# A two-layer hybrid trunk on one core: recurrence gates in blocks of 80 channels, rotated scores stacked in float32r, another order of steps

## The chip, the cores and the metric

The kernel runs on one core of one Trainium2 chip. The metric is device time in microseconds (us) of one launch, the median over the runs shown. The profile is one execution of the program, taken by the hardware profiler.

Engines go by the profile's names: PE is TensorE (matrix products; PEld is its loading of the stationary operand), DVE is VectorE, ACT is ScalarE, POOL is GpSimd and SP is SyncE, whose queue issues nearly all DMAs of this kernel.

## The reference

Two layers act on 256 tokens of 1024 channels. In each, one large projection of the normed input feeds three mixers (a gated MLP over positions, attention with 8 heads, a linear recurrence), and their outputs are gated, projected, merged and added to the input:

```python
def mla_attention(c_q, c_kv, k_rope_in, ...):        # per head: 128 plain + 64 rotated channels
    ...
    q = jnp.concatenate([q_nope, q_rope], axis=-1)
    k = jnp.concatenate([k_nope, broadcast(k_rope)], axis=-1)
    s = jnp.einsum('bqhd,bkhd->bhqk', qi, k) * scale   # masked by chunks, softmax, times v
...
def rg_lru(x_c, conv_w, conv_b, w_a, b_a, w_x, b_x, lam):
    xc = depthwise_conv(x_c, conv_w) + conv_b             # 1280 channels, width 4
    xb = xc.reshape(B, S, 16, 80)                         # 16 blocks of 80 channels
    r = sigmoid(einsum('bshi,hij->bshj', xb, w_a) + b_a)
    i = sigmoid(einsum('bshi,hij->bshj', xb, w_x) + b_x)
    a = exp(-8 * r * softplus(-lam))
    h = scan(a, sqrt(1 - a*a) * i * xc)                   # h[t] = a[t] h[t-1] + b[t]
...
for l in range(2):
    h = rmsnorm(x); proj = h @ w_in[l]
    ...
    merged = sig(g_a) * (y_a @ w_proj_a) + sig(g_b) * (y_b @ w_proj_b) + sig(g_c) * (y_c @ w_proj_c)
    x = x + rmsnorm(merged @ w_out[l])
```

## The kernel before, in words

**Number format.** A float32 product is made of float32r products: each operand is split into a rounded high part (an ACT copy, `act(hi, src, AF.Copy)`) and a rest (a DVE subtraction), and `mm3` issues three products, high by high, high by low and low by high. Plain float32 operands go to PE unsplit in the scores and in the products with the softmax weights.

**Weights.** The weights are cut into chunks, mostly 1 MB (1024 rows by 256 columns, 48 products of 256 moving columns on PE). `load` issues a chunk's DMA on SP into one of three `raw` buffers; `split` makes `whi` and `wlo` from it in one of three pairs. When a step has used its chunk, `done` (through `fin`) gives the pair back, and `pump` splits the next chunk into it and issues the load of the third chunk after that. So PE has up to two split chunks ahead of the one it uses, and up to three more are loaded or loading.

**The order.** All steps of a layer stand in the table `ORDER`; the program is issued in just that order on every engine, with no rearrangement. `LATE` says at which point inside a step the chunk is given back. A step name has a number: `("ga", 2)` is the third chunk of gate a. The names that matter here: `xc` projects the recurrence's input, `conv` convolves it, `split` and `stack` prepare it for the gates, `la` and `lx` make its gates r and i, `r1`, `r2`, `r3` are the recurrence itself; `uq` and `ukv` make queries, keys and values, `attend i` issues the scores of heads 2i and 2i+1 and the later parts of the two pairs before; `u`, `za`, `zb`, `zc`, `ga` to `gc` and `pa` to `pc` are the other projections; `v` and `norm` belong to the gated MLP.

**The scores.** A head's scores take, for queries 0 to 127 (128 keys) and for queries 128 to 255 (256 keys), one float32 product of the plain part (`q`, `k`) and one of the rotated part (`qr`, `krt`). `qr` holds two heads over 128 partitions, and the two `krt` tiles have zeros where the other head's channels are.

**The gates.** The 1280 channels lie in two groups of five tiles of 128 partitions, which the blocks of 80 don't match. So `load` puts the blocks piece by piece (16 DMAs per chunk, after a POOL memset) into a sparse band of weights, and `lru_gate` covers each tile of 128 outputs by one full `mm3` plus either one product over 96 stacked partitions or another `mm3`. `conv_stack` copies the needed edges of the split input into `xs` and `xm`, on DVE, ACT and POOL. A step `la` or `lx` has 24 products of 256 columns; a layer has four such steps.

PSUM is used as a ring of five banks `mm` and one of three `aux`; small temporaries are a ring of eight tiles `t`; larger ones are 16 slots taken in turn.

## Time and profile before

| | |
|---|---|
| median of 3 runs | 798.14 us (798.09 to 798.59) |
| the profiled execution: time, span of its instructions | 798.34 us, 796.6 us |
| PE busy, DVE busy, ACT busy, POOL busy | 788.1, 548.9, 469.3, 70.5 us |
| granted TensorE clock, mean | 0.997 |
| moved by DMA, mean rate | 137.87 MB, 173 GB/s |
| written to HBM | 1.05 MB |

Busy times are sums over the instructions of an engine; instructions on PE overlap, so that the time of one product is read from the distance of two starts and not from its duration. In the rows below, a line number such as L731 is one of the kernel before; a row of a float32 (not float32r) product counts two records for one instruction.

### The profile page before, as it was taken

The numbers are of one execution on the slowest core, as the hardware profiler recorded it, in microseconds if no ns is written. First come the engines' busy times: TensorE is split into PE (matmuls) and PEld (weight loads), VectorE is DVE, ScalarE is ACT, GpSimd is POOL, SyncE is SP. The second block draws the span as 40 slices with busy tenths as digits, with TensorE's granted clock in tenths as the row PEclk, the third lists the DMA queues.
The fourth block names the chain that finished last, engine by engine and source line by source line (L and its number), as shares of the span: only waits on it lengthen the run. The fifth ranks groups of instructions, "written<-read, shape, count | busy, mean of one in ns | idle before, by whom it ended". The sixth has DMA issues, their size and how long they took to land.

```text
span 796.6 us, 15355 instructions
## 1 busy us (share of the span) xinstructions
PE 788.1 (99%) x6445; PEld 780.2 (98%) x6445; DVE 548.9 (69%) x712; ACT 469.3 (59%) x689; POOL 70.5 (9%) x110
## 2 busy tenths in 40 slices
PE   9999999999999999999999999999999999999996
PEld 8999999999999999999999999999999999999996
DVE  5587788666876787555666868776578578775562
ACT  5785767339855736343567776654595584544441
POOL 1100503003000000000010032031210000000000
PEclk9999999999999999999999999999999999999998
DMA  7845454344666565666357626541575656564531
GB/s 229 290 152 182 153 161 155 112 122 137 201 213 211 159 215 169 199 212 216 109 171 239 208 94 211 159 128 51 166 219 167 221 162 202 185 214 150 193 132 54
DMA packets 134205, 137.87 MB, mean 173 GB/s; under 512 B 11046, under 2 KB 130808, under 8 KB 134136
## 3 DMA queue, kind: packets, MB, share of 16 engines
q1 hardware_dynamic: 134120, 136.90, 54.3%
q8 instruction: 50, 0.82, 0.4%
q14 instruction: 19, 0.16, 0.1%
q10 hardware_dynamic: 16, 0.00, 0.0%
HBM read 135.83 MB, written 1.05 MB: 172 GB/s over the span
## 4 chain that ended last, share of the span: by engine, by line
PE 94%; DMA 2%; issue 1%; DVE 1%; ACT 1%; SPq 0%; POOL 0%; POOLq 0%; DVEq 0%; ACTq 0%
PE mm L308 25%; PE mm L307 25%; PE mm L309 25%; PE mm L431 2%; PE mm L433 2%; PE mm L432 2%; DMA raw<-in_w_in_dram 1%; PE aux L843 1%; PE mm L730 1%; PE aux L770 1%; PE mm L731 1%; DMA X<-in_x_dram 1%; PE mm L549 1%; PE aux L1021 1%; PE mm L1020 1%
## 5 line engine op out<-in xcount | busy, mean ns | idle before, releaser
L269 DVE TENSOR_TENSOR wlo<-raw,whi 128x2048 fp32r<-128x2048 f32 (+5 forms) x123 | 264.6, 2156 | 115.9 <-ACT whi L268 115.5
L307 PE MATMUL mm<-hT,whi 128*128 128x256 f32 x1088 | 307.1, 282 | 0.0
L309 PE MATMUL mm<-hT,wlo 128*128 128x256 f32 x1088 | 305.8, 281 | 0.3 <-DVE wlo L269 0.3
L308 PE MATMUL mm<-hT,whi 128*128 128x256 f32 x1088 | 305.6, 281 | 0.0
L268 ACT ACTIVATE whi<-raw 128x2048 fp32r<-128x2048 f32 (+5 forms) x123 | 221.0, 1802 | 66.6 <-PE mm L308 26.8
L309 PEld LDWEIGHTS mm<-hT,wlo 128*128 128x128 f32 x1088 | 205.0, 188 | 0.5 <-DVE wlo L269 0.5
L307 PEld LDWEIGHTS mm<-hT,whi 128*128 128x128 f32 x1088 | 205.0, 188 | 0.0
L308 PEld LDWEIGHTS mm<-hT,whi 128*128 128x128 f32 x1088 | 205.0, 188 | 0.0
L973 ACT ACTIVATE t<-mm 128x512 f32<-128x512 f32 x18 | 10.8, 598 | 52.2 <-PE mm L309 52.2
L397 POOL TENSOR_TENSOR rstd<-rstd,mhalf 128x1 f32<-128x1 f32 x8 | 4.4, 551 | 391.1 <-DVE rstd L396 391.1
L308 PE MATMUL mm<-yc,whi 128*128 128x256 f32 x128 | 36.0, 282 | 0.0
L308 PE MATMUL mm<-ya,whi 128*128 128x256 f32 x128 | 36.0, 282 | 0.0
L307 PE MATMUL mm<-ya,whi 128*128 128x256 f32 x128 | 36.0, 281 | 0.0
L307 PE MATMUL mm<-yc,whi 128*128 128x256 f32 x128 | 36.0, 281 | 0.0
L431 PE MATMUL mm<-whi,hT 128*128 128x256 f32 x128 | 36.0, 281 | 0.0
L308 PE MATMUL mm<-yb,whi 128*128 128x256 f32 x128 | 35.9, 281 | 0.0
L309 PE MATMUL mm<-ya,wlo 128*128 128x256 f32 x128 | 35.9, 280 | 0.0
L309 PE MATMUL mm<-yc,wlo 128*128 128x256 f32 x128 | 35.9, 280 | 0.0
L309 PE MATMUL mm<-yb,wlo 128*128 128x256 f32 x128 | 35.8, 280 | 0.0
L307 PE MATMUL mm<-yb,whi 128*128 128x256 f32 x128 | 35.8, 280 | 0.0
L432 PE MATMUL mm<-wlo,hT 128*128 128x256 f32 x128 | 35.8, 279 | 0.0
L433 PE MATMUL mm<-whi,hT 128*128 128x256 f32 x128 | 35.7, 279 | 0.0
(279 smaller groups left out, 1663.4 us busy)
## 6 DMA issues: line engine op xcount, KB each, us to landing
raw<-in_w_in_dram SPq DMA_DIRECT2D x76, 1024.0 KB
raw<-in_w_proj_a_dram SPq DMA_DIRECT2D x8, 1024.0 KB
raw<-in_w_proj_b_dram SPq DMA_DIRECT2D x8, 1024.0 KB
raw<-in_w_proj_c_dram SPq DMA_DIRECT2D x8, 1024.0 KB
raw<-in_w_out_dram SPq DMA_DIRECT2D x8, 1024.0 KB
raw<-in_mla_w_uq_dram SPq DMA_DIRECT2D x8, 576.0 KB
raw<-in_mla_w_ukv_dram SPq DMA_DIRECT2D x4, 1024.0 KB
raw<-in_w_in_dram SPq DMA_DIRECT2D x4, 640.0 KB
```

What stands on the lines that cost most here:

```text
L268: act(hi[:, w], c.raw[:, w], AF.Copy)
L269: V.tensor_tensor(lo[:, w], c.raw[:, w], f(hi[:, w]), ALU.subtract)
L307: mm(ps, lh, rh, start=start, stop=False)
L308: mm(ps, lh, rl, start=False, stop=False)
L309: mm(ps, ll, rh, start=False, stop=stop)
L431: mm(ps, lh, rh, start=k == 0, stop=False)
L432: mm(ps, lh, rl, start=False, stop=False)
L433: mm(ps, ll, rh, start=False, stop=k == KT - 1)
L549: mm(ps, ll, rh, start=False, stop=j % 2 * 4 + k == KT - 1)
L730: mm(sc[:, P : 3 * P], qn[:, P:], kn, start=True, stop=False)
L731: mm(sc[:, P : 3 * P], qp[:, P:], kr, start=False, stop=True)
L973: act(sg, ps, AF.Sigmoid)
```

## The change

There are four parts.

- **Gates by blocks.** A chunk `lg` now has four blocks of 80 channels of both `w_a` and `w_x`. The split input is stored to DRAM tiles (`split`, now one ACT copy, one DVE subtraction and two stores) and read back by blocks (`stack`): 80 high rows and, under them, 48 low rows of the block in one tile; the 80 high rows again and the other 32 low rows in a second. Each block then takes two products, over 128 and over 112 partitions, with 80 output rows. The biases go into the sigmoid of 80 partitions, from a layout by blocks; the sigmoids are stored to DRAM as well, and the new step `in` reads them back in tiles of 128 channels for `r1`. Weights come by six DMAs per chunk, of 80, 48 and 48 rows by 4 by 80, without a memset.
- **Scores.** The rotated query of a head is kept as 64 high and 64 low rows of one float32r tile (`qr`, now two tiles of four heads; two ACT copies and two DVE subtractions more in each `uq` step), and the key as two float32r tiles: `krt[0]` has its high part twice, `krt[1]` its rest twice. The rotated float32 product becomes two float32r products.
- **Order.** `ORDER` is rewritten: four steps `lg` in place of `la` and `lx`, `in` after every second one, and other places for `conv`, `split`, `stack`, `attend`, `zc`, `gb` and `pc`.
- **Constants.** The bias rows are loaded by 16 blocks of 80; the `rows` tile is cleared from row 64 on POOL.

```diff
 ORDER = (
-    ("wl", 0), ("xc", 0), ("turn", 0), ("xc", 1), ("conv", 0), ("uq", 0), ("conv", 1), ("xc", 2), ("ukv", 0),
...
+    ("xc", 0), ("wl", 0), ("turn", 0), ("xc", 1), ("conv", 1), ("uq", 0), ("conv", 0), ("xc", 2), ("xc", 3),
...
+    ("split", 1), ("pa", 0), ("ga", 1), ("lg", 1), ("in", 0), ("pa", 1), ("ga", 2), ("stack", 2), ("pa", 2),
+    ("r1", 0), ("ga", 3), ("r2", 0), ("pa", 3), ("zb", 0), ("stack", 3), ("lg", 2), ("zb", 1), ("zb", 2),
+    ("zb", 3), ("r3", 0), ("gb", 0), ("pb", 0), ("lg", 3), ("in", 1), ("gb", 2), ("gb", 1), ("pb", 1), ("r1", 1),
+    ("r2", 1), ("pb", 2), ("zc", 0), ("zc", 1), ("rows", 0), ("r3", 1), ("zc", 2), ("zc", 3), ("zc", 4), ("gc", 0),
...
 def load(c, parts=1, mid=None):
...
+        l, g = c.lru
+        for i, x in enumerate("ax"):
+            at = slice(i * WH, (i + 1) * WH)
+            w = I["lru_w_" + x][l, g * NH : (g + 1) * NH].rearrange("b r c -> r b c")
+            r1, r2 = v2(c.raw[:, at], BW), v2(c.raw[:, W2 + i * WH : W2 + (i + 1) * WH], BW)
+            nc.sync.dma_start(r1[:BW], w)
+            nc.sync.dma_start(r1[BW:], w[:K1])
+            nc.sync.dma_start(r2[64 : BW + K2], w[K1 - (BW - 64) :])
...
         if c.lru:
+            raw, r2 = c.raw[:, :W2], c.raw[64 : BW + K2, W2 : 2 * W2]
+            act(hi[:, :W2], raw, AF.Copy)
+            act(lo[64 : BW + K2, :W2], r2, AF.Copy)
+            V.tensor_tensor(lo[:BW, :W2], raw[:BW], f(hi[:BW, :W2]), ALU.subtract)
...
 def turn_ranks(_):
-                            act(krt[0][:64], o[:64], AF.Copy)
-                            act(krt[1][64:], o[:64], AF.Copy)
+                            for r in (slice(0, HR), slice(HR, P)):
+                                act(krt[0][r], o[:HR], AF.Copy)
+                                V.tensor_tensor(krt[1][r], o[:HR], f(krt[0][:HR]), ALU.subtract)
...
 def queries(j):
-                V.tensor_tensor(qr[:, j], qa[:, :S], qs[:, :S], ALU.add)
+                V.tensor_tensor(qa[:, :S], qa[:, :S], qs[:, :S], ALU.add)
                 fin(c, "uq", 3)
+                for a in range(2):
+                    own, other = (slice(i * HR, (i + 1) * HR) for i in (a, 1 - a))
+                    to = qr[j // 2][:, j % 2 * 2 + a]
+                    act(to[own], qa[own, :S], AF.Copy)
+                    V.tensor_tensor(to[other], qa[own, :S], f(to[own]), ALU.subtract)
...
+            def conv_split(g):
+                cv[g] = [xc[g]]
+                for w in ("xh", "xl"):
+                    x = slot(w, (GT, S), F32R)
...
+                    d = dp.tile([GT * P, S], F32, tag=f"{w}{g}", name=nm(w))
+                    nc.sync.dma_start(d.rearrange("(k p) s -> p k s", p=P), f(x))
+            def conv_stack(h):
...
+                bh, bl = (d[rows].rearrange("(b r) s -> r b s", r=BW) for d in (dh, dl))
+                st2[h] = [slot("xs", (NH, S), F32R) for _ in range(2)]
+                for x, b in zip(st2[h], (bl[:K1], bl[K1:])):
+                    nc.sync.dma_start(f(x[:BW]), bh)
+                    nc.sync.dma_start(f(x[BW : BW + b.shape[0]]), b)
...
 def scores(i):
-                    mm(sc[:, 0:P], qp[:, 0:P], kr[:, 0:P], start=False, stop=True)
-                    mm(sc[:, P : 3 * P], qp[:, P:], kr, start=False, stop=True)
+                        mm(o, qp[:, ts], krt[0][:, :n], start=False, stop=False)
+                        mm(o, qp[:, ts], krt[1][:, :n], start=False, stop=True)
...
+            def lru_gates(h):
+                x1, x2 = st2[h]
+                c = get(l, "lg", h)
...
+                    for b0 in range(0, NH, 2):
+                        ps, o = bank(), tmp()
+                        for b in (b0, b0 + 1):
...
+                            mm(pb, wh[:, ws], x1[:, b], start=True, stop=False)
+                            mm(pb, wl[: BW + K2, ws], x2[: BW + K2, b], start=False, stop=True)
...
+                            act(o[:BW, bs], ps[:BW, bs], AF.Sigmoid, bias=pt[:BW, r : r + 1])
+                        nc.sync.dma_start(rows[:, b0 : b0 + 2], v2(o[:BW], S))
+                fin(c, "lg", 1)
+            def gate_in(g):
+                for key in ("la", "lx"):
+                    o = slot(key, (GT, S))
+                    nc.sync.dma_start(o, gates[key, g].rearrange("(k p) s -> p k s", p=P))
+                    gates[key, g] = o
```

The following rows give the instructions as they stand on an engine: line, operation, output and inputs (with buffer numbers), and the shape of the output. No time is in them.

On PE, in the first `attend` of the first layer, two heads before the change (`mm` is a PSUM bank of scores):

```order
L728 MATMUL mm_83<-k_385,q_383 128x128
L729 MATMUL mm_83<-krt_105,qr_389 128x128
L730 MATMUL mm_83<-k_385,q_383 128x256
L731 MATMUL mm_83<-krt_105,qr_389 128x256
L728 MATMUL mm_84<-k_385,q_383 128x128
L729 MATMUL mm_84<-krt_106,qr_389 128x128
L730 MATMUL mm_84<-k_385,q_383 128x256
L731 MATMUL mm_84<-krt_106,qr_389 128x256
```

and the same two heads after it:

```order
L715 MATMUL mm_87<-k_385,q_383 128x128
L716 MATMUL mm_87<-krt_107,qr_389 128x128
L717 MATMUL mm_87<-krt_108,qr_389 128x128
L715 MATMUL mm_87<-k_385,q_383 128x256
L716 MATMUL mm_87<-krt_107,qr_389 128x256
L717 MATMUL mm_87<-krt_108,qr_389 128x256
L715 MATMUL mm_83<-k_385,q_383 128x128
L716 MATMUL mm_83<-krt_107,qr_389 128x128
L717 MATMUL mm_83<-krt_108,qr_389 128x128
```

The plain products (L728 and L730, now L715) stay; each product with `krt` becomes two, of the same shape.

On PE, the first gate step of the first layer before the change (the start of `la`; two tiles of 128 outputs):

```order
L307 MATMUL mm_84<-xh_1406,whi_94 128x256
L308 MATMUL mm_84<-xl_1407,whi_94 128x256
L309 MATMUL mm_84<-xh_1406,wlo_95 128x256
L927 MATMUL mm_84<-xs_1469,whi_94 128x256
L307 MATMUL mm_84<-xh_1406,whi_94 128x256
L308 MATMUL mm_84<-xl_1407,whi_94 128x256
L309 MATMUL mm_84<-xh_1406,wlo_95 128x256
L307 MATMUL mm_84<-xs_1469,whi_94 128x256
L308 MATMUL mm_84<-xm,whi_94 128x256
L309 MATMUL mm_84<-xs_1469,wlo_95 128x256
```

and the first `lg` step after it (two products for each block, from the two `xs` tiles):

```order
L757 MATMUL aux_88<-t_82,vv_388 128x128
L906 MATMUL mm_85<-xs_1441,whi_94 80x256
L907 MATMUL mm_85<-xs_1442,wlo_95 80x256
L906 MATMUL mm_85<-xs_1441,whi_94 80x256
L907 MATMUL mm_85<-xs_1442,wlo_95 80x256
L906 MATMUL mm_86<-xs_1441,whi_94 80x256
L907 MATMUL mm_86<-xs_1442,wlo_95 80x256
```

An `lg` step goes on like this through four banks, 16 products in all, and stands behind the last products of `attend 5` (the L757 row); a layer has 64 of them where it had 96.

On SP, what is queued around `lg 1` and `in 0` of the first layer after the change (`t` are the sigmoids, `la` and `lx` the DRAM tiles and, as targets of the L918 rows, the tiles read back):

```order
L192 DMA raw_93<-in_w_in_dram 128x8x256
L192 DMA raw_91<-in_w_proj_a_dram 128x8x256
L911 DMA la_1944<-t_79 80x2x256
L911 DMA la_1944<-t_80 80x2x256
L911 DMA lx_1959<-t_81 80x2x256
L911 DMA lx_1959<-t_82 80x2x256
L192 DMA raw_92<-in_w_in_dram 128x8x256
L918 DMA la_2179<-la_1944 128x5x256
L918 DMA lx_2181<-lx_1959 128x5x256
L201 DMA raw_93<-in_lru_w_a_dram 80x4x80
L202 DMA raw_93<-in_lru_w_a_dram 48x4x80
L204 DMA raw_93<-in_lru_w_a_dram 48x4x80
```

Before the change SP had here only loads of weights; now four stores that wait for ACT, and two loads that wait for those stores to land, stand between the weight loads, in the one queue.

## The prediction

> **What bounds the kernel now.** I read the page first (busy times, the chain that ended last), then the waits, then PE's timeline in the two places that the change rewrites, then SP's.

> ```profile
> PE 788.1 (99%) x6445; PEld 780.2 (98%) x6445; DVE 548.9 (69%) x712; ACT 469.3 (59%) x689; POOL 70.5 (9%) x110
> PE 94%; DMA 2%; issue 1%; DVE 1%; ACT 1%; SPq 0%; POOL 0%; POOLq 0%; DVEq 0%; ACTq 0%
> PE mm L309 <- DVE wlo L269: 0.3, 1, 0.3
> SPq L200 <- DVE wlo L269: 392.7, 78, 12.2
> ```

> PE is busy for 99% of the span and carries 94% of the chain; the third row, the whole wait of PE's products for split weights, is one wait of 0.3 us. SP, on the contrary, waits half of the span for splits before it may load: loads come when buffers are free. So a product that is taken from PE shortens the run by its pace on PE, and any other work counts only if it makes PE wait.

> **The pace of a product on PE.** The distances of starts in PE's timeline, in the first `attend` and in the last tiles of the first `lx`:

> ```profile
> 70.88 0.38 PE L728 MATMUL mm<-k,q 128*128 128x128 f32 x2
> 71.10 0.39 PE L729 MATMUL mm<-krt,qr 128*128 128x128 f32 x2
> 71.32 0.60 PE L730 MATMUL mm<-k,q 128*128 128x256 f32 x2
> 71.75 0.59 PE L731 MATMUL mm<-krt,qr 128*128 128x256 f32 x2
> 72.19 0.38 PE L728 MATMUL mm<-k,q 128*128 128x128 f32 x2
> 182.17 0.28 PE L307 MATMUL mm<-xh,whi 128*128 128x256 f32 x1
> 182.53 0.28 PE L927 MATMUL mm<-xs,whi 96*128 96x256 f32 x1
> 182.65 0.28 PE L307 MATMUL mm<-xh,whi 128*128 128x256 f32 x1
> 185.02 0.28 PE L307 MATMUL mm<-ya,whi 128*128 128x256 f32 x1
> 187.38 0.28 PE L309 MATMUL mm<-ya,wlo 128*128 128x256 f32 x1
> ```

> A float32 product holds PE for 0.22 us at 128 moving columns and for 0.43 at 256; a head's scores take 72.19 - 70.88 = 1.31 us. A `la` or `lx` step is 24 products between 182.17 and 185.02, 2.85 us, 0.119 each; the chunk behind it goes at 0.118 (185.02 to 187.38 is 20 products). The product over 96 partitions takes 0.12 like the others, so the number of rows sets no time.

> **The gates.** Eight steps of 2.85 us go: -22.8 us. Two layers by 64 products of 256 columns come: 128 x 0.118 = +15.1. Only the 80 stationary columns are new in them; the bounds of their pace are 0.109 (a transpose, shown next) and 0.119, which is 14.0 to 15.2. I take 0.118, since 256 columns still move. Net -7.7 us (-8.8 to -7.6).

> **The scores.** Per head, 0.22 + 0.43 = 0.65 us of rotated float32 products go; two float32r products of 256 columns (2 x 0.118 = 0.236) and two of 128 columns come. No float32r product of this kernel moves fewer than 256 columns, so the last has to be bounded. Below: half of the 256-column pace, 0.059 (the 512-column product of the next fence, 0.23, is twice the 256-column one, so the pace follows the columns). Above: the 0.22 us that a float32 product of 128 columns takes, if a short float32r product is run in as many passes. Between them stand the transposes, 128 columns in one record:

> ```profile
> 85.92 0.65 PE aux L759 x6
> 53.27 0.23 PE mm L667
> ```

> Six take 0.65 us, 0.109 each; a float32 record of 128 columns is 0.11 too. Every record with 128 columns in this trace goes at that pace, so I take 0.109: 0.236 + 0.218 = 0.454 in place of 0.65, -0.2 us per head, 16 heads, -3.3 us. The ends are -4.8 us (16 x (0.65 - 0.354)) and 0 (0.236 + 0.44 is 0.68, +0.4 at the worst). [...]

> **Sum.** 798.34 (the profiled execution; the span is 796.6 and 1.7 lie around it) - 7.7 - 3.3 = 787.3. The median of the runs is 0.2 below that execution: 787.1, taken as 787.2.

> **What I cost at nothing, and its cover.** ACT, DVE and POOL change little:

> ```profile
> L932 ACT ACTIVATE la<-mm,pt 128x256 f32<-128x256 f32 x16 | 6.2, 479 | 0.0
> L447 ACT ACTIVATE xs<-xl 32x256 fp32r<-32x256 f32 (+1 forms) x16 | 6.2, 413 | 0.2
> L260 ACT ACTIVATE whi<-raw 128x1280 fp32r<-128x1280 f32 x8 | 10.2, 1270 | 2.5 <-PE mm L308 2.4
> L643 ACT ACTIVATE t<-mm 32x256 f32<-32x256 f32 x32 | 12.0, 376 | 0.8 <-PE mm L309 0.3
> L449 DVE CAST xs<-xh 64x512 fp32r<-64x512 f32 x8 | 4.0, 495 | 0.1
> L647 DVE TENSOR_TENSOR qr<-t,t 128x256 f32<-128x256 f32 x8 | 3.5, 438 | 0.3
> ```

> ACT: 64 sigmoids of 80 rows in place of 40 (24 x 0.48 = +11.5), 16 copies for `qr` (x 0.376 = +6), less 24 `xs` copies (x 0.41 = -10); the gate weights keep two copies per chunk, of half of L260's width: at most +7 us of 796. DVE: 16 subtractions for `qr` and 4 for `krt` (20 x 0.44 = +9) against 16 edge copies (x 0.49 = -8) and shorter gate splits: about 0. POOL loses its copies and memsets. The cover is the two split chunks that PE has ahead, 2 x 48 x 0.118 = 11.3 us; without it these few us would show one for one.

> SP issues 128 DMAs in both layers in place of the gate weights' 128 small ones, but they carry a new load: the stores and loads through DRAM, per layer 2.62 MB (`xh`, `xl`), 3.93 (`xs`), 2.62 and 2.62 (gates out and back), 23.6 MB for both.

> ```profile
> q1 hardware_dynamic: 134120, 136.90, 54.3%
> 154.16 9.20 SPq L210 DMA_DIRECT2D raw<-in_lru_w_a_dram  x16
> 163.46 7.72 SPq L210 DMA_DIRECT2D raw<-in_lru_w_x_dram  x16
> 171.28 0.39 SPq L200 DMA_DIRECT2D raw<-in_w_proj_a_dram  x1
> 155.00:163.00 8.00, 8.00 (x70) 8.00 (x70) 3.92 (x4) 4.17 (x3) 1.17 (x1) 1.00 0.16 28
> 310.00:330.00 20.00, 20.00 (x171) 20.00 (x170) 13.28 (x12) 9.19 (x9) 0.00 (x0) 1.00 0.81 257
> ```

> 136.90 MB for 54.3% of 796.6 us is 316 GB/s at full share (the last row agrees, 257 / 0.81 = 317). The added 23.6 MB take 75 us of it, so the share rises to some 64%. The SP rows show how much delay the loads can bear: from 154 to 171 us SP issues nothing but 32 tiny DMAs, and PE stays busy all through. The chunk loaded at 171.28 is first used at 185.02 (L307 on `ya`), 13.7 us later, of which load (3.3), ACT copy and DVE subtraction (1.8 and 2.3, next rows) take 7.4.

> ```profile
> L268 ACT ACTIVATE whi<-raw 128x2048 fp32r<-128x2048 f32 (+5 forms) x123 | 221.0, 1802 | 66.6 <-PE mm L308 26.8 <-issue 26.3 <-DMA raw<-in_w_in_dram 8.9
> L269 DVE TENSOR_TENSOR wlo<-raw,whi 128x2048 fp32r<-128x2048 f32 x108 | 248.0, 2299 | 112.4 <-ACT whi L268 112.2
> ```

> The waits that the change puts on SP are for ACT's sigmoids, for the `xh` and `xl` splits, for earlier readers of a slot, and for stores to land. The weight load queued behind each waits for a later split anyway (392.7 us above), so only landings are new delay. The tightest place is between the first `lg` and `r1 0`: PE has six chunks of 48 products and `lg 1` there, 6 x 5.65 + 1.9 = 35.8 us, and DMA must move six chunks (6.29 MB), 2 x 0.655 MB of sigmoids out and 1.31 back, 1.31 of `xh` and `xl` and 0.98 of `xs`, 11.2 MB or 35.4 us at 316 GB/s, and 0.45 MB of gate weights in rows of 320 bytes, 2.6 us at the 28 / 0.16 = 175 GB/s of the 155:163 row: some 38 us. That is 2 us over, against some 6 of spare lead: no wait, but little to spare. Between the second pair, `lg 2` to `r1 1`, 47 us of PE stand against 41.

> The start keeps its chain (the loads stand in the same order on SP); the tail behind the last product is untouched.

> **Rivals.**
> (1) Short float32r products take as many passes as float32, the upper bound above. Then only the gates gain: 798.14 - 7.7 = 790.4. Against it, the 128-column record at 0.109; for it, float32's 0.22. It decides from 0.2 us per product.
> (2) Late sigmoids, small waits. `r2 1` now follows `r1 1` at once and only `pb 2` follows before `zc`: table, exponentials and tanh (rows below, 1.28 + 5 x 0.50 + 5 x 0.50), two DVE passes of 1.48 and 0.83, another table and root (1.28 + 1.27), then the next weight split, 1.8 + 2.3: it ends about 14 us behind the start of `r1` (the second table loads while DVE works), and PE wants it at 16.9 (three chunks). So 3 us of lateness of the read-back gates are free and each further one costs 1 us at up to four places; 1 to 2 us at each give 791 to 795, and small ones alone 789.

> ```profile
> L942 ACT ACTIVATE a<-la,sA 128x256 f32<-128x256 f32 x20 | 8.4, 498 | 0.0
> L944 ACT ACTIVATE la<-la,sT 128x256 f32<-128x256 f32 x20 | 8.4, 495 | 0.0
> L953 ACT ACT_TABLE_LOAD x4 | 5.1, 1283 | 0.1
> L953 ACT ACTIVATE u<-u 128x1280 f32<-128x1280 f32 x4 | 5.1, 1274 | 14.8 <-DVE u L952 14.8
> L951 DVE SCALAR_TENSOR_TENSOR u<-u,la 128x1280 f32<-128x1280 f32 x4 | 5.9, 1483 | 0.0
> HBM read 135.83 MB, written 1.05 MB: 172 GB/s over the span
> ```

> (3) Slower: DMA falls behind in the tight stretch of each layer, because stores to DRAM go slower than loads, or because the landing waits leave the engines empty. The last row shows that the trace says nothing of the rate of stores: 1.05 MB were written. At 250 GB/s the stretch needs 44.8 + 2.6 = 47.4 us, 5.6 more than the 35.8 and the 6 spare ones; two layers lose 11 us and the gain is gone: that is the point from which it decides. At 220, between 316 and the 175 of the short rows, it needs 53.5, and 2 x 11.7 = 23 us are lost: 810. Against it stands 316. [...]

> **How the numbers follow.** The forecast (785 to 789, short products between 0.059 and 0.12, next to no waits) has 50 in 100; rival 1 has 21; rival 2 has 16; rival 3 has 13, of which 5 end within 0.2% and 8 slower. 0.2%, 1.6 us, is about what a measurement of this kernel can tell from no change. All but rival 3 are faster: 87, 5 and 8. The range 784.5 to 793 holds the forecast, rival 1 and most of rival 2, about 82.

> **What would show it.** PE busy near 777 us and still about 99%; 0.45 us for the rotated products of a head (0.68 in rival 1); an `lg` step of 1.9 us; DMA share near 64% with slices near full from the first `lg` to `r1 0`; no wait of PE above 1 us. It is wrong if the list of waits has PE behind `whi`, `wlo` or `xs`, or ACT and DVE behind a DMA of `la` or `lx` for several us.

## The result, and the profile after

The changed kernel takes 790.09 us (788.26 to 790.67, four executions) beside 798.12 us for the kernel before: a ratio of 0.9895, 95% interval 0.9878 to 0.9913, 8.0 us faster. The forecast was 787.2 us, with a range of 784.5 to 793.

Lines of the page after (the profiled execution took 790.08 us, its span is 788.3 us):

```profile
PE 778.4 (99%) x6381; PEld 771.4 (98%) x6381; DVE 540.4 (69%) x708; ACT 472.3 (60%) x705; POOL 39.2 (5%) x78
PE 96%; issue 2%; DMA 1%; ACT 1%; DVE 0%; SPq 0%; POOLq 0%; POOL 0%; DVEq 0%; ACTq 0%
q1 hardware_dynamic: 162584, 162.45, 66.5%
```

PE still bounds the kernel. It is busy for 9.7 us less (788.1 before), yet the span is only 8.3 us shorter: the difference is in waits. These are PE's, from the list of waits (engine, line, what it waited for: us in total, times, longest), besides the 1.0 us in which the warm-up waits for its operand, in both kernels:

```profile
PE mm L521 <- ACT hT L477: 1.2, 1, 1.2
PE mm L281 <- ACT t L861: 1.0, 2, 0.5
PE mm L523 <- DVE hT L479: 0.5, 1, 0.5
```

The third stood in the profile before too. The first is new and lies at the start of the program, the second is new and lies behind the second gate step of each layer. No wait of PE is for a DMA.

**The scores.** PE's timeline in the first `attend` (start, duration, line):

```profile
75.24 0.38 PE L715 MATMUL mm<-k,q 128*128 128x128 f32 x2
75.38 0.30 PE L716 MATMUL mm<-krt,qr 128*128 128x128 f32 x1
75.52 0.28 PE L717 MATMUL mm<-krt,qr 128*128 128x128 f32 x1
75.63 0.65 PE L715 MATMUL mm<-k,q 128*128 128x256 f32 x2
75.93 0.47 PE L716 MATMUL mm<-krt,qr 128*128 128x256 f32 x1
76.23 0.28 PE L717 MATMUL mm<-krt,qr 128*128 128x256 f32 x1
76.35 0.38 PE L715 MATMUL mm<-k,q 128*128 128x128 f32 x2
```

A head takes 76.35 - 75.24 = 1.11 us, where it took 1.31. Its part with 128 moving columns (75.24 to 75.63) takes 0.39 us, where it took 0.44 (70.88 to 71.32 in the prediction's rows); its part with 256 columns (75.63 to 76.35) takes 0.72, where it took 0.87. The three products of a part share its time in a way that these starts don't separate: L717 is followed after 0.11 us, L716 after 0.14, and the plain product, which held PE for 0.22 before, after 0.14.

**The gates.** PE at the end of the first layer's second `lg` step and at the next step's first product, then ACT at the same time:

```profile
192.53 0.28 PE L906 MATMUL mm<-xs,whi 128*80 128x256 f32 x1
194.34 0.28 PE L907 MATMUL mm<-xs,wlo 112*80 112x256 f32 x1
195.11 0.39 PE L281 MATMUL mm<-ya,whi 128*128 128x256 f32 x1 [0.50 <-ACT t L861]
```

```profile
192.66 1.92 ACT L242 ACTIVATE whi<-raw 128x2048 fp32r<-128x2048 f32 x1 [3.71 <-PE mm L282]
194.48 0.58 ACT L861 ACTIVATE t<-mm 128x512 f32<-128x512 f32 x1
```

The 16 products go at 0.12 us each, 1.9 us in all. Then the first product of `pa 1` should start at 194.46 and starts at 195.11, 0.65 us late. Its PSUM bank is that of `ga 1`, two steps before, and the sigmoid of `ga 1` (L861), which empties the bank, stands in ACT's queue behind a split copy of 1.92 us: `LATE` has `ga` give its chunk back, and so issue that copy, before its sigmoid. The same happens in the second layer.

**The start.** PE from its warm-up products to the second set of transposes, and a window (time, PE busy with its count, ..., granted clock, DMA share, GB/s), first of the kernel before, then of the changed kernel:

```profile
0.99 6.33 PE L479 MATMUL aux<-ones 128*128 128x128 f32 x28 [0.99 <-POOL ones L457]
11.69 2.05 PE L499 MATMUL aux<-t,X 128*128 128x128 f32 x16
12.00:14.00 2.00, 2.00 (x19) 2.00 (x18) 1.53 (x4) 1.16 (x6) 0.00 (x0) 1.00 0.71 202
```

```profile
0.97 5.12 PE L453 MATMUL aux<-ones 128*128 128x128 f32 x28 [0.97 <-POOL ones L433]
9.62 0.45 PE L521 MATMUL mm<-whi,hT 128*128 128x384 f32 x1 [1.17 <-ACT hT L477]
11.75 3.52 PE L473 MATMUL aux<-t,X 128*128 128x128 f32 x16
12.00:14.00 2.00, 2.00 (x10) 2.00 (x11) 1.59 (x4) 0.24 (x2) 0.00 (x0) 0.50 0.73 216
```

In this execution the 28 warm-up products took 5.12 us instead of 6.33. PE was then done early with the first transposes and idle for 1.17 us until their copies came from ACT. The ranks begin as late as before (9.62 us; 9.55 before), so the idle time itself cost nothing. But the granted clock fell to 0.50 behind it, and 16 transposes took 3.52 us in place of 2.05. The first product of 256 columns starts at 29.69 us; before, at 28.01.

**DMA.** The window from the first `lg` on, before and after:

```profile
180.00:220.00 40.00, 40.00 (x340) 40.00 (x339) 29.97 (x25) 35.91 (x49) 8.74 (x9) 1.00 0.54 165
```

```profile
180.00:220.00 40.00, 39.50 (x335) 39.26 (x333) 25.24 (x20) 25.17 (x33) 0.00 (x0) 1.00 1.01 302
```

The 16 DMA engines are full for 40 us at 302 GB/s, and PE loses 0.5 us there, which is the bank.

**The account of this execution**, from the last product (789.70 before, 781.79 after; -7.9 us) and from the distances of starts summed over all gate products and all score products: gates 22.84 to 16.86 us, -6.0 (with the two bank waits, 1.3); scores 20.95 to 17.84, -3.1; start +1.7; the rest -0.5, which was not traced further. In the profile of `after_again`, below, the gates and scores are the same to the hundredth, the start is -0.1, and the last product starts at 780.61: 9.1 us earlier than before, with nothing left over.

### The profile page after: what moved, and what is told of

Its sections match the earlier page's. It is cut to its first block, busy times and chain, and to the rows that moved or that the text cites. A ratio compares the mean times of both kernels' runs of the same rounds, so it can differ in the third digit from the quotient of the medians.

```text
span 788.3 us, 15228 instructions
## 1 busy us (share of the span) xinstructions
PE 778.4 (99%) x6381; PEld 771.4 (98%) x6381; DVE 540.4 (69%) x708; ACT 472.3 (60%) x705; POOL 39.2 (5%) x78
## 3 DMA queue, kind: packets, MB, share of 16 engines
q1 hardware_dynamic: 162584, 162.45, 66.5%
## 4 chain that ended last, share of the span: by engine, by line
PE 96%; issue 2%; DMA 1%; ACT 1%; DVE 0%; SPq 0%; POOLq 0%; POOL 0%; DVEq 0%; ACTq 0%
PE mm L281 24%; PE mm L282 24%; PE mm L283 24%; PE mm L409 2%; PE mm L407 2%; PE mm L408 2%; PE mm L715 1%; PE mm L523 1%; PE mm L521 1%; PE mm L522 1%; PE aux L829 1%; PE aux L756 1%; DMA X<-in_x_dram 1%; PE mm L907 1%; PE mm L906 1%
## 5 line engine op out<-in xcount | busy, mean ns | idle before, releaser
L242 ACT ACTIVATE whi<-raw 128x2048 fp32r<-128x2048 f32 (+5 forms) x123 | 221.0, 1802 | 90.4 <-PE mm L282 71.2
L428 ACT ACTIVATE mg<-acc 128x512 fp32r<-128x512 f32 x8 | 5.1, 632 | 42.8 <-DVE acc L881 42.8
```

Of the source, the lines that this page charges most:

```text
L242: act(hi[:, w], c.raw[:, w], AF.Copy)
```

## The experiments

Each has its interval of the ratio to the kernel before, run beside it. PE's first 256-column product tells how the start went.

| kernel | median us | ratio (interval) | 28 warm-up products, us | idle before the ranks | clock 12 to 14 us | first 256-column product |
|---|---|---|---|---|---|---|
| before (first profile) | 798.12 | | 6.33 | 0 | 1.00 | 28.01 |
| changed (first profile) | 790.09 | 0.9895 (0.9878 to 0.9913) | 5.12 | 1.17 | 0.50 | 29.69 |
| after_again | 788.68 | 0.9878 (0.9865 to 0.9892) | 6.15 | 0 | 1.00 | 27.95 |
| ga_sigmoid_first | 791.32 | 0.9908 (0.9895 to 0.9922) | 5.33 | 0.93 | 0.50 | 29.81 |
| warm5 | 788.53 | 0.9872 (0.9857 to 0.9887) | 5.85 | 0 | 1.00 | 28.60 |
| scores_f32 | 793.77 | 0.9935 (0.9923 to 0.9947) | 5.11 | 1.83 | 0.50 | 30.16 |
| lg_aux | 788.57 | 0.9865 (0.9850 to 0.9880) | 4.77 | 1.68 | 0.50 | 29.69 |
| scores_only | 806.10 | 1.0081 (1.0066 to 1.0096) | 5.01 | 1.06 | 0.50 | 29.50 |
| order_only | 798.96 | 1.0002 (0.9993 to 1.0011) | 6.02 | 0 | 1.00 | 27.88 |
| xs_twice | 817.76 | 1.0227 (1.0205 to 1.0249) | 5.83 | 0 | 1.00 | 27.87 |
| scores_order | 796.51 | 0.9972 (0.9961 to 0.9983) | 4.92 | 0.80 | 1.00 | 27.85 |
| xs_extra | 789.14 | 0.9883 (0.9863 to 0.9904) | 5.38 | 1.46 | 0.50 | 30.23 |
| warm_short | 790.16 | 0.9885 (0.9865 to 0.9905) | 4.34 (20 products) | 1.39 | 0.50 | 29.87 |
| lg_aux_warm5 | 786.90 | 0.9852 (0.9832 to 0.9872) | 5.70 | 0 | 1.00 | 28.31 |

### The start: after_again, warm5, warm_short

`after_again` is the changed kernel, unchanged.

> The changed kernel, unchanged, beside the same runs of the kernel before. The span is expected at 788 to 789 us and the time near 790. Theory S (the clock at the start is a matter of the run): the granted clock between 10 and 16 us differs from the first profile's 0.86, 0.50, 0.79, and the first product of 256 columns starts earlier than 29.69 us where the clock is higher. Rival C (the new code itself slows the start): the same three windows and 29.69 again.

```profile
0.97 6.15 PE L453 MATMUL aux<-ones 128*128 128x128 f32 x28 [0.97 <-POOL ones L433]
11.48 2.05 PE L473 MATMUL aux<-t,X 128*128 128x128 f32 x16
```

788.68 us, span 787.1: theory S. The same program, with a warm-up of 6.15 us, kept its clock and had its first 256-column product at 27.95, as the kernel before had. So the 1.7 us belong to the execution, not to the change; how long the 28 warm-up products take varies between 4.8 and 6.3 us over the table, with the old steps and the new.

```diff
             first_turn(0, d0, bank, lambda: ds.append(diagonal(r)))
-            warm(1)
+            warm(5)
```

> The changed kernel with five warm-up products in place of one between the first transposes and the ranks (some 0.9 us of TensorE work put into its idle time near 8 to 10 us). Theory G (the idle there lowers the granted clock and costs 1.5 us at half pace): the clock stays at 1.00 between 10 and 16 us, the first product of 256 columns starts 1 to 1.7 us earlier, and the run is about 1.5 us faster than the changed kernel. Rival (the clock there has nothing to do with that idle, or the products only add): within 0.3 us, or up to 0.9 us slower.

788.53 us (788.17 to 788.95). The profile has the clock at 1.00 and no idle time. Beside `after_again` that is no measurable gain, since three of that kernel's four executions took under 789 us as well; what is gone are those near 790 (four of the changed kernel's eight took 789.8 to 790.7). The profile does not show the added products at work: its warm-up took 5.85 us, and `xs_twice`, with 5.83 us and one warm-up product at this place, has no idle time either. That they help rests on the executions: four here and five of `lg_aux_warm5`, none of which is far behind the others (they spread over 0.8 and 1.2 us).

```diff
-        warm(14)
+        warm(10)
```

> The changed kernel with 20 warm-up records at the start in place of 28. Theory (an idle TensorE between the first transposes and the ranks lowers the granted clock for some 3.5 us): the idle is over 1 us in every run, the clock falls to 0.5 between 10 and 16 us, and the times are those of the changed kernel's slower executions, 789.9 to 790.7. Rival (the clock falls for another reason, the warm-up being too long rather than too short): 788.5 or less.

```profile
9.73 0.44 PE L521 MATMUL mm<-whi,hT 128*128 128x384 f32 x1 [1.39 <-ACT hT L477]
12.00:14.00 2.00, 2.00 (x10) 2.00 (x11) 1.70 (x5) 0.24 (x2) 0.00 (x0) 0.50 0.79 239
```

The median is 790.16 and the profile shows idle and drop as expected; but "in every run" was too much: of five executions one took 787.71 us and one 789.45. Over the table the link holds without exception: each of the seven profiles with an idle stretch of 0.93 us or more has the clock at 0.50 and a first 256-column product at 29.5 to 30.2 us, and each of the seven with 0.80 or less has 1.00 and 27.9 to 28.6. By an estimate the clock stays down for some 3.4 us (in the first profile after, three windows of 2 us, from 10 to 16 us, have 0.86, 0.50 and 0.79: lost are 0.28, 1.00 and 0.42 us, 1.7 in all, which at a clock of 0.50 is 3.4 us), and 1.7 us is what the start lost. That the idle causes the drop is the likeliest reading of these 14 profiles, not a proof: what else differs from one execution to the next was not varied.

### The bank: ga_sigmoid_first, lg_aux

```diff
-LATE = {"ga": 1, "gb": 1, ...
+LATE = {"ga": 0, "gb": 1, ...
```

> The changed kernel with the gate steps' sigmoids issued at once, ahead of the next weight split in ScalarE's queue. Theory (the 0.65 us that the first product of the step behind the second gate step starts late comes from its PSUM bank, which a sigmoid behind a 1.9 us split copy frees): both stalls vanish, 1.3 us less than the changed kernel, unless the split behind the sigmoids becomes late. Rival (another cause, for instance the split weights): the stall stays at 0.65 us and the time within 0.3 us.

```profile
PE mm L906 <- DVE acc L883: 2.8, 2, 1.4
230.80 0.68 DVE L883 TENSOR_TENSOR acc<-t,mm 128x512 f32<-128x512 f32 x1
231.53 0.34 PE L906 MATMUL mm<-xs,whi 128*80 128x256 f32 x1 [1.36 <-DVE acc L883]
```

The wait for L861 is gone, which the rival excluded, and the kernel is slower: 791.32 us. The new wait lies in `lg 2` of each layer. In ACT's queue the sigmoid of `ga 3`, with a table load of 1.28 us, now stands ahead of the split copies for `lg 2`; the splits that follow on ACT and DVE come 1.2 us later. Behind them DVE reaches `pa 3`'s product with its gate (L883) at 230.80, and the fourth bank of `lg 2` is `pa 3`'s: PE waits 1.4 us for it. The stall was moved, not mended.

```diff
-                        ps, o = bank(), tmp()
+                        ps, o = (aux if b0 else bank)(), tmp()
```

> The changed kernel with every other PSUM bank of an lg step taken from the ring of three auxiliary banks instead of the ring of five, so that the step behind the second lg no longer comes round to the bank of the gate step before it. ScalarE's and SyncE's order is unchanged. Theory (TensorE waits there for that bank): the two waits of 0.5 us for the sigmoid of L861 vanish with nothing in their place, some 1.3 us less than the changed kernel, 787.4 us in runs with a good start. Rival (ScalarE is late there whatever the bank): the wait moves to the next step, as it did when the sigmoid was put first, and the time is that of the changed kernel or 1 to 2 us more.

PE at the same place:

```profile
194.34 0.28 PE L907 MATMUL aux<-xs,wlo 112*80 112x256 f32 x1
194.46 0.28 PE L281 MATMUL mm<-ya,whi 128*128 128x256 f32 x1
```

The product starts 0.12 us behind the last gate product, the waits for L861 have left the list, and nothing takes their place. All gate products now take 15.56 us in place of 16.86: 1.3, as expected. The median, 788.57 us, does not show it alone, since in the profiled execution at least the start was of the bad kind (idle 1.68 us, clock 0.50); from the first 256-column product to the last this kernel needs 750.5 us, the changed one 752.1.

### The scores and the order: scores_f32, scores_only, order_only, scores_order

`scores_f32` takes the changed kernel back to float32 scores.

```diff
-                        mm(o, qp[:, ts], krt[0][:, :n], start=False, stop=False)
-                        mm(o, qp[:, ts], krt[1][:, :n], start=False, stop=True)
+                        mm(o, qp[:, ts], krt[a][:, :n], start=False, stop=True)
```

> The changed kernel with the rotated part of the scores in float32 again, 16 heads. Theory (the gain of the scores is 0.2 us a head, all of it from the 256-column half, since two short float32r products at 0.11 take what one of float32 took): 3.1 to 3.3 us slower than the changed kernel. Rival (short float32r products are no faster in the end, or the scores are covered by other waits): less than 1 us slower.

793.77 us, 5.1 more than `after_again`. Of the 5.0 between the two profiled executions 2.2 are the start (30.16 against 27.95). The score products take 20.55 us against 17.84: 2.7. That is some 0.4 too little, because in two places the float32r product behind the scores has its start recorded 0.2 us early (20.95 in the kernel before, where a float32 product follows). From the first 256-column product to the last product the step is 755.5 against 752.7 and 752.1 us in the changed kernel's two profiles: 2.8 to 3.4, as large as expected, and the rival is out. It does not all come from the 256-column part, though: that gives 0.15 us a head and the other 0.05.

`scores_only` is the kernel before with the new scores, in the old order.

> The kernel before with only the new scores: the rotated parts stacked in float32r, two products in place of one float32 product. Forecast's step: 16 heads x 0.2 us = 3.3 us faster; by the distances of the changed kernel 3.1. Rival (a short float32r product costs what float32 costs): 0 to 0.5 us slower.

```profile
PE aux L762 <- DVE t L754: 6.0, 2, 3.1
ACT qr L651 <- DVE t L646: 7.4, 4, 3.3
```

Both missed: 806.1 us, 7 slower, although the score products take 17.85 us as in the changed kernel. In each layer PE stands 3 us before the transposes of the fourth pair of heads, and behind that idle the clock falls again (0.91 as the mean of 120 to 140 us). The late engine is DVE:

```profile
125.39 0.56 DVE L741 TENSOR_REDUCE max<-mm 128x3 f32<-128x384 f32 x1
127.03 0.37 ACT L748 ACTIVATE t<-mm,max 128x128 f32<-128x128 f32 x1 [3.55 <-DVE max L742]
```

PE begins the last score product of that pair at 118.44 us. DVE takes the first row maximum at 125.39, and the exponentials on ACT wait for it. In the old order DVE has `conv 3` and `conv 4` in front of `uq 3` and its softmax, and now the new subtractions too. The new ACT copy of the rotated query waits up to 3.3 us for DVE (the second of the two rows further up), and what stands behind it in ACT's queue waits with it. The cost of the added work is more than the 7 us: the score products gain 3.1, so it is about 10, of which the two stops of PE are 6. The clock behind the first of them is some 1.8 us, an estimate from 0.91 over 20 us; with as much behind the second it would be most of the rest.

`order_only` is the kernel before, arithmetic and all, with its steps in the new order.

> The kernel before with its own steps put in the changed kernel's order (la and lx where lg 1 and lg 3 stand). Theory (the order itself gains nothing, the arithmetic does): 798 us, within 1 us of the kernel before. Rival (the order is part of the gain): 2 us or more faster; or it needs the new gates to be fed and is 2 us or more slower.

798.96 us, ratio 1.0002: the order by itself gains nothing.

`scores_order` has the new scores and the new order, with the old gates.

> The kernel before with the new scores and the changed kernel's order, but its own gates. Theory (the 6 us that TensorE waited for the softmax, when the new scores stood in the old order, come from the place of the query steps in ScalarE's and VectorE's queues, and the new order takes them away): 3.1 us faster than the kernel before, no wait of the transposes for L754. Rival (the extra copies and subtractions cost VectorE this wherever they stand, and the new gates hid it): still 3 us or more slower than the kernel before.

```profile
ACT qr L650 <- DVE t L645: 1.5, 4, 0.4
```

The busy times from 90 to 126 us (PE, PEld, DVE, ACT, POOL) of the kernel before, of `scores_only` and of `scores_order`:

```profile
90.00:126.00 36.00, 36.00 (x291) 35.29 (x290) 28.89 (x59) 24.20 (x52) 3.61 (x7) 1.00 0.62 201
90.00:126.00 36.00, 36.00 (x298) 35.59 (x297) 31.13 (x60) 22.99 (x47) 5.45 (x9) 1.00 0.56 174
90.00:126.00 36.00, 36.00 (x297) 35.54 (x296) 26.44 (x53) 25.51 (x59) 11.69 (x16) 1.00 0.57 176
```

796.51 us, 2.3 faster (interval of the ratio 0.9961 to 0.9983, 1.4 to 3.1 us). The four waits of ACT shrink from 7.4 to 1.5 us, and PE waits for no softmax. In the new order `conv 3` and `conv 4` stand behind `uq 3` and its softmax, and DVE has 26.4 us of work in this stretch instead of 31.1. So the order is worth nothing alone and about 9 us to the new scores (from 1.0081 to 0.9972). Which of its moved steps does it was not run: that it is the two convolutions is argued from DVE's queue.

### The margin of DMA: xs_twice, xs_extra

```diff
-                for x, b in zip(st2[h], (bl[:K1], bl[K1:])):
+                for x, b in [xb for xb in zip(st2[h], (bl[:K1], bl[K1:])) for _ in range(2)]:
```

> The changed kernel with every load of the stacked rows issued twice: 3.93 MB more per layer, near the place that the prediction called tight. Theory (DMA has spare lead there, as its list of waits without a DMA says): within 0.5 us of the changed kernel. Rival 3 of the prediction (stores and loads run DMA short between the first lg and r1 0): at 250 to 316 GB/s each layer has 12 to 16 us more to move, and beyond the spare lead TensorE waits for split weights, 5 to 20 us slower.

```profile
SPq L699 <- DMA xs<-xh: 71.0, 16, 7.0
200.00:204.00 4.00, 4.00 (x21) 4.00 (x20) 1.14 (x1) 2.83 (x4) 0.00 (x0) 0.50 1.07 377
```

817.76 us, 29 more than the changed kernel in `after_again`, beyond the rival's worst. But here a load that writes the rows of the load before it waits until that has landed, and SP stood 71 us for it, with the weight loads queued behind. PE then waited for late sums and copies (19.6 us over its list) and went on at half clock (21 products started in 4 us, with the clock at 0.50, where the changed kernel started 36 in the same window at 1.00). So this run alone can't tell bandwidth from queue.

`xs_extra` moves the same bytes with nobody waiting.

```diff
                     nc.sync.dma_start(f(x[BW : BW + b.shape[0]]), b)
+                    for n, s in enumerate((bh, b)):
+                        e = dp.tile([BW, NH * S], F32, tag=f"e{h}{n}{b.shape[0]}", name=nm("e"))
+                        nc.sync.dma_start(v2(e[: s.shape[0]], S), s)
```

> The changed kernel with 3.93 MB more DMA traffic per layer that nobody waits for: each block of rows that is loaded for the stack is also copied to an unused place in DRAM, in the same position of SyncE's queue. It tells apart why the doubled loads cost 29 us. Bandwidth theory (the stretch from the first lg to r1 0 has no spare DMA time): 15 to 30 us slower again. Queue theory (the second load of the same rows had to wait for the first to land and held SyncE for 71 us in all, while DMA itself has several us to spare): less than 10 us slower.

```profile
180.00:220.00 40.00, 39.50 (x334) 39.26 (x334) 24.74 (x20) 25.20 (x32) 0.00 (x0) 1.00 1.04 318
```

789.14 us, ratio 0.9883: the same as the changed kernel, with 7.9 MB more and no wait of PE for a DMA. The queue theory holds: the 29 us came from SP held by landings, not from the number of bytes. (These copies end in DRAM and not in SBUF; that the writes to SBUF were the limit in `xs_twice` was not run apart, but the 377 GB/s above speaks against it.) How large the margin of the bytes is stays open, since only one of the four copied blocks of a layer, 0.98 MB or 3.1 us at 316 GB/s, is issued at the head of the tight stretch, and the next at its end. Of rival 3's two mechanisms, slow stores did not show; landing waits are real, and the changed kernel merely has little of them (9.6 us of SP's time for the gates' stores, in five waits).

### Both mends: lg_aux_warm5

> Both mends together: the lg step's second bank from the auxiliary ring, and five warm-up products in place of one between the first transposes and the ranks. Theory (1.3 us of bank waits and, in the runs whose warm-up ends early, 1 to 2 us at the start): about 787.2 us, and a span near 785.5, 1.3 less than with the warm-up products alone. Rival (what is won at one place is given back at the next): 788.5.

PE's list of waits without the wait for the warm-up's operand, and its line on the page:

```profile
PE mm L523 <- DVE hT L479: 0.5, 1, 0.5
PE 777.6 (99%) x6389; PEld 771.3 (98%) x6389; DVE 540.4 (69%) x708; ACT 472.6 (60%) x705; POOL 39.9 (5%) x78
```

786.90 us (786.34 to 787.57), span 785.3, as expected. It beats both kernels: every execution lies below every one of `warm5` and of the changed kernel, and it is 11.9 us below the kernel before (ratio 0.9852). `warm5` ran beside other executions of the kernel before, and the two intervals of the ratio overlap; from the first 256-column product to the last, the profiles have 750.6 us here and 752.1 in `warm5`.

## Why the prediction was right, and where it was off

The sign, the bound (PE) and the mechanism (fewer and shorter products on PE, nearly everything else hidden) were right, and the time lay in the range. It lay 2.9 us above the forecast, and outside the 785 to 789 given to the likeliest case; in the second measurement (788.68) it lay inside. Step by step:

- **Gates, -7.7 forecast, -6.0 measured.** The 128 products were put at 0.118 us; without the bank wait (`lg_aux`) they take 15.56 us, 0.122 each, just above the upper bound of 0.119: 0.4 us. The other 1.3 us are the bank wait, twice 0.65. "No wait of PE above 1 us" failed only at the start (1.2 us), but "next to no waits" left out that a step of 1.9 us between two of 5.7 comes round to a PSUM bank before ACT's queue has reached the sigmoid that empties it. The prediction followed ACT's load, not its order against the ring.
- **Scores, -3.3 forecast.** -3.1 by the account, -2.8 to -3.4 between `scores_f32` and the changed kernel, -2.3 in the time of `scores_order`. The sum is right, its two terms are not, and that they cancel is luck: the 128-column part of a head was to gain nothing (0.22 against 0.218) and gains 0.05, the 256-column part was to gain 0.19 and gains 0.15. So 0.109 as the pace of a short product is not confirmed: if the plain product still holds PE for 0.22, the two short ones take 0.085 each and the two long ones 0.145, an estimate from 0.39 and 0.72. Rival 1 is wrong: it needs 0.66 us for the 128-column part. The pace of a single short product stays open. Nor did every record with 128 columns go at 0.109 in the kernel before: the 28 of its warm-up took 6.33 us, 0.226 each.
- **The start, 0 forecast, +1.7 in the profiled execution.** "The start keeps its chain" is true of the order, and false of the clock. The kernel before very likely has the same weakness: `scores_only`, which keeps its order of steps, shows the drop (29.50). The kernel before itself has no profile with the drop: its one profile showed the good case, and the forecast set off from that.
- **ACT and DVE, costed at nothing.** Right for the whole change. But the cover that was named, two split chunks, is not what hides the extra copies and subtractions: PE stopped for a softmax, not for a split weight, and with the old order this work cost about 10 us, 7 after the gain of the scores. The new order, which the prediction gave no value, is what hides it.
- **DMA.** A share of 66.5% for 64 forecast, full engines in the tight stretch as forecast, no wait. The stretch was forecast 2 us over PE's time, with 6 us of lead; `xs_extra` put some 3 us more into it, and PE waited for no DMA.
- **Rival 2** came in its mildest form and at another place: not late read-backs at `r1` or `r2`, but the bank behind `lg 1`.

## What to carry to other kernels

Where one engine is full and the others work through their queues in the program's order, price a new small operation by what stands in front of it and behind it in its queue, not by its duration: here the same copies and subtractions cost about 10 us in one order and 1 or less in another. When a step gets much shorter, go round the buffer rings with it and ask who empties the buffer that the step after it needs; here another ring mended the wait (1.3 us), and another order only moved it (1.4 us at the new place). Here 1.17 us of idle on PE cost no time of its own and went with 1.7 us lost at a lower granted clock, so it is worth trying to fill such a gap with idle products.
